# Stick-breaking weights as differences of suffix products, one weight tile per query tile in place, and transposed weights in ring slots

## The chip, the cores and the metric

One Trainium2 chip, of which this kernel uses one core. The metric is the time of one execution on the device in microseconds, as the median over runs. A core has five engines that run their own instruction streams in order: TensorE (PE, with its weight loads shown as PEld), VectorE (DVE), ScalarE (ACT), GpSimd (POOL) and SyncE (SP, which here issues all DMAs).

## The reference

One layer of a hybrid encoder. A prompt group of 1,024 tokens and a sample group of 32 tokens (with caches of 512 keys) go through the same weights. Each token is normed and projected to q, k, v and gate for two mixers of 8 heads x 64 each; mixer A is a softmax over a band, mixer B is stick-breaking attention. All is float32.

```python
def band_attention(q, k, v, q_pos, k_pos, bias_table):          # mixer A
    s = jnp.einsum('bqhd,bkhd->bhqk', q, k).astype(jnp.float32) * ATTN_SCALE
    rel = jnp.clip(k_pos[None, :] - q_pos[:, None], -REL_CLIP, REL_CLIP) + REL_CLIP
    s = s + bias_table[:, rel].astype(jnp.float32)[None]
    ok = ...                                # own 64-token chunk and the 8 before it
    w = jax.nn.softmax(jnp.where(ok[None, None], s, NEG_INF), axis=-1)
    return jnp.einsum('bhqk,bkhd->bqhd', w, v)

def stick_breaking(q, k, v, q_pos, k_pos):                      # mixer B
    z = jnp.einsum('bqhd,bkhd->bhqk', q, k).astype(jnp.float32) * ATTN_SCALE
    causal = (k_pos[None, :] < q_pos[:, None])[None, None]
    log_beta = jax.nn.log_sigmoid(z)
    log_1m = jnp.where(causal, jax.nn.log_sigmoid(-z), 0.0)
    after = lax.cumsum(log_1m, axis=3, reverse=True) - log_1m
    w = jnp.where(causal, jnp.exp(log_beta + after), 0.0)
    return jnp.einsum('bhqk,bkhd->bqhd', w, v)

def finish(h, oa, ga, ob, gb, w_out, g_post, p, w_ple, w_ple_gate):
    y = jnp.concatenate([oa * jax.nn.silu(ga), ob * jax.nn.silu(gb)], axis=-1) @ w_out
    h = h + rmsnorm(y, g_post)
    return h + jax.nn.sigmoid(h @ w_ple_gate) * (p @ w_ple)
```

In mixer B the weight of key k is sigmoid(z_k) times the product of sigmoid(-z_j) over all later keys j. With S_k the suffix product of sigmoid(-z_j) over j >= k, that weight is also S_(k+1) - S_k, because sigmoid(z) = 1 - sigmoid(-z).

## The kernel before

Every float32 operand of a matmul is split into a high part in fp32r and a low part (the rest), and each product is made of two or three fp32r matmuls. The work runs in these steps:

1. Up to about 66 us: the inputs are normed and turned, an early part of the per-layer embedding is made, and the first head pair's q, k and v columns are projected.
2. From there to about 600 us: 8 stages, one for each pair of heads, in the order A0 B0 A1 B1 A2 B2 A3 B3. A stage weaves two streams: the attention of its pair (two heads, named for instance A00 and A01) and "dense" work, which is the projection of the next stage's columns (`mm_kB1` are the k columns of pair B1) and, in the last stage, of all gates. The sample group's attention (`PVsA0`, `PVsB0`, ...) is put into the stages of odd pairs.
3. After that the output projection and the gate product, each by a Strassen-like scheme.

A head's attention works on 8 query tiles of 128. For tile i, `scores(i)` multiplies q with the keys into one or two PSUM banks of tag "S" (three banks) and makes the weights: for B, DVE adds the causal mask, ACT takes sigmoid(-z) into `w0` (ring `om`) and sigmoid(z) into `w1` (ring `be`), DVE scans `w0` from the right to suffix products, and POOL multiplies the two; for A, DVE adds the bias and takes the maximum into `w0`, ACT takes the exponential into `w1`, and POOL normalises it. `weights_t(i)` comes two tiles later: PE transposes the 128x128 blocks of `w1` into banks of tag "T" (two banks), ACT copies the high part to `wTh`, DVE the low part to `wTl`. Tiles 4 and 6 of each A head (`ROUND`) are turned by DVE and DMAs through a scratch in DRAM instead, and come back in four DMAs of 32 partitions each. `values(g)` then multiplies the values with the turned weights of four query tiles (g is 0 or 1; PV of tag "PV", one bank); its moving operand is a `Segments`, one run of 128 columns for each query tile. The sample's value product uses the same PV bank and keeps its operands in the four slots of tag "wr", into which the dense work's next weight columns are loaded as well.

`Arena` hands out columns of one big buffer in turn; a new tile waits for every user of the tiles that it overlaps. `wTh` and `wTl` are such rings of 33 x 128 columns, with one tile for each group of four query tiles.

None of this is the order on the chip. All operations go to a `Recorder` first, which notes for each what it must wait for: an operation on a view waits for earlier ones on an overlapping box of the same buffer. `Recorder.order` then lays out each engine's queue by simulating the kernel with estimated durations: whenever an engine is free it takes, of what is ready, the operation with the lowest key; attention's matmuls (class 0) go before dense ones (class 1). An operation on SP counts as landed some time after its issue. What a view knows of its box:

```python
    def rearrange(self, pattern, **sizes):
        ...
        return View(self.buf, self.steps + (("rearrange", pattern, sizes),), self.box, [None] * len(shape), shape)
```

A rearranged view keeps the box that it had, and an index into it afterwards doesn't make the box smaller, since its dimensions are None.

Almost every instruction is issued from one place of the recorder, so the profile gives them all line 450; they are told apart by the names of their tiles.

Of the kernel before, what the change touches and what calls it, by code (L numbers as in the profile page):

```python
# [8 lines left out]
F32 = mybir.dt.float32  # L9
# [21 lines left out]
ROUND = {"A": ((4,),(6,)), "B": ()}  # L31
# [127 lines left out]
class Segments:  # L159


    def __init__(self, buf, start, step, n):
        self.buf, self.start, self.step, self.n = buf, start, step, n
        self.shape = [buf.shape[0], n, P]
        self.box = (buf.box[0], (start, start + (n - 1) * step + P))

    def get(self):
        base = self.buf.get()[:, self.start:self.start + P]
        return bass.AP(tensor=base.tensor, offset=base.offset, ap=[base.ap[0], [self.step, self.n], [1, P]])
# [83 lines left out]

class Engine:
# [9 lines left out]
class Recorder:  # L264
# [43 lines left out]
    def add(self, eng, what, args, kw):  # L308
        writes, reads = [], []
        method = what[1] if isinstance(what, tuple) else ""  # L310
        for i, a in enumerate(args):
            if isinstance(a, (View, Raw, Segments)):
                (writes if i == 0 or (method == "tensor_tensor_reduce" and i == 7) else reads).append(a)
        for k, a in kw.items():
            if isinstance(a, (View, Raw, Segments)):
                (writes if k in ("out", "accum_out") else reads).append(a)
        o = self.node(eng, what, args, kw, set())
        for mine, write in ((reads, False), (writes, True)):
            for v in mine:
                b = v.buf  # L320
                hit = False
                for other, box, wrote in b.uses:
                    if other is not o and (write or wrote) and all(p < y and x < q for (p, q), (x, y) in zip(v.box, box)):
# [6 lines left out]
                b.uses.append((o, v.box, write))  # L330
        o.busy, o.late = self.cost(eng, method, args, kw, writes, reads)
        o.shared = eng == "POOL"
        if eng == "DVE":
            sbuf = [v for v in reads if isinstance(v, (View, Segments)) and not v.buf.psum and v.free() > 4]
            o.shared = len(sbuf) > 1 or (method == "tensor_copy" and len(sbuf) == 1 and not writes[0].buf.psum)

    @staticmethod
    def cost(eng, method, args, kw, writes, reads):
# [3 lines left out]
        psum = any(isinstance(v, (View, Segments)) and v.buf.psum for v in reads)  # L342
# [97 lines left out]
    def emit(self, tc):  # L440
        ops = self.order()
        with tc.manual_schedule():
            for o in ops:
# [3 lines left out]
                args = [a.get() if isinstance(a, (View, Raw, Segments)) else a for a in o.args]  # L447
                kw = {k: a.get() if isinstance(a, (View, Raw, Segments)) else a for k, a in o.kw.items()}
# [7 lines left out]
def stream_step(  # L456
# [58 lines left out]
    ringh, ringl = (Arena(rec, at, x, 33 * P, F32R) for x in ("wTh", "wTl"))  # L515
# [26 lines left out]
    def ensure(j):  # L542
# [6 lines left out]
        if j == 2:  # L549
            pair = [ringl.tile([P, 2, 4, P], f"w{x}_{kind}{p}") for x in "hl"]  # L550
# [14 lines left out]
    def load_x(t):  # L565
        n = min(P, T - t * P)
        if t == 3:
            x34.append(at.tile([P, ringh.cols], F32, tag="wTh", name="x34")[:, 0:2 * D].rearrange("p (a c) -> p a c", a=2))
# [209 lines left out]
    def attention(ab, p, h):  # L778
# [15 lines left out]

        together = {i: g for g in ROUND[ab] for i in g}
        whole, done_with = {}, []

# [3 lines left out]
        def rooms(i):  # L801

            more = ab == "B"
            g = together.get(i, (i,))
            if g not in whole:
                n = sum(cost(x) for x in g) * P
                whole[g] = ring0.tile([P, n + more * len(g)], f"om{nm}_{i}"), ring1.tile([P, n], f"be{nm}_{i}")
            k, n = g.index(i), cost(i) * P
            a = sum(cost(x) for x in g[:k]) * P
            w0, w1 = whole[g]  # L810
            return w0[:, a + more * k:a + more * k + n + more], w1[:, a:a + n]

        def scores(i):
# [5 lines left out]
            w0, w1 = rooms(i)  # L819
# [8 lines left out]
            if ab == "B":  # L828
# [3 lines left out]
                nc.gpsimd.memset(w0[:, n:n + 1], 1.0)  # L832
                for a, b, s in pieces:
                    nc.scalar.activation(w0[:, a:b], s, AF.Sigmoid, scale=-1.0)
                for a, b, s in pieces:
                    nc.scalar.activation(w1[:, a:b], s, AF.Sigmoid)
                for a, b, s in reversed(pieces):
                    rev = w0[:, a + 1:b + 1][:, ::-1]
                    nc.vector.tensor_tensor_scan(rev, rev, s, 1.0 if b == n else w0[:, b + 1:b + 2], ALU.mult, ALU.bypass)
                nc.gpsimd.tensor_tensor(w1[:, 0:n], w1[:, 0:n], w0[:, 1:n + 1], ALU.mult)  # L840
            else:
                m = small.tile([P, 4], F32, tag="stat", name=f"stat{nm}_{i}", bufs=6)
                for j, (a, b, s) in enumerate(pieces):
                    nc.vector.tensor_tensor_reduce(
                        w0[:, a:b], s, box["bias"][:, n - b:n - a][:, ::-1], 1.0,
# [6 lines left out]
            state[i] = w0, w1  # L852

        wT = {}
# [5 lines left out]
        def weights_t(i):  # L860
            g = i // 4
            step, size = LAID[ab, g]
            if g not in wT:
                wT[g] = [x.tile([P, size * P], f"{x.name}{nm}_{g}") for x in (ringh, ringl)]
            b0 = lo_block(i)
            w0, w1 = state.pop(i)
            n = i + 1 - b0
            at_ = ((i - 4 * g) * step + b0) * P
            hi, lo = (x[:, at_:at_ + n * P] for x in wT[g])
            if i in together:  # L870

                group = together[i]
                done_with.append((i, hi, lo))
                if i != group[-1]:
                    return
                w0, w1 = whole[group]
                m = sum(cost(x) for x in group)
                first = {x: sum(cost(y) for y in group[:k]) for k, x in enumerate(group)}
                squares = w0[:, 0:m * P].rearrange("p (c b q) -> p b c q", c=4, q=32)
                for x, _, _ in done_with:  # L880
                    y = slice(first[x], first[x] + cost(x))
# [6 lines left out]
                turned = w1.rearrange("p (g b q) -> p g b q", g=4, q=32)  # L888
                for x, hi, lo in done_with:
                    src = turned[:, :, first[x]:first[x] + cost(x), :]  # L890
                    hi, lo = (y.rearrange("p (b g q) -> p g b q", g=4, q=32) for y in (hi, lo))
                    nc.scalar.copy(hi, src)
                    nc.vector.tensor_tensor(lo, src, f(hi), ALU.subtract)
                done_with.clear()
                return
            for b in range(0, n, 4):
                m = min(4, n - b)
                pt = psum("T", f"ptw{nm}_{i}_{b}")
                for x in range(m):
                    nc.tensor.transpose(pt[:, x * P:(x + 1) * P], w1[:, (b + x) * P:(b + x + 1) * P], ident)  # L900
                c = slice(b * P, (b + m) * P)
                nc.scalar.copy(hi[:, c], pt[:, 0:m * P])
                nc.vector.tensor_tensor(lo[:, c], pt[:, 0:m * P], f(hi[:, c]), ALU.subtract)
# [6 lines left out]
        def values(g):  # L910
# [36 lines left out]
    def sample_attention(ab, gi):  # L947
# [44 lines left out]
        def scores():  # L992
# [6 lines left out]
            w0 = ring0.tile([P, NK + 1], "w0" + nm)  # L999
            w1 = ring1.tile([P, NK], "w1" + nm)  # L1000
            if ab == "B":
                new = pieces[1][2][:, NK // 2 - NS:NK // 2]
                nc.vector.tensor_tensor(new, new, masks, ALU.add)
                nc.gpsimd.memset(w0[:, NK:NK + 1], 1.0)
                for a0, b0, s in pieces:
                    nc.scalar.activation(w0[:, a0:b0], s, AF.Sigmoid, scale=-1.0)
                for a0, b0, s in pieces:
                    nc.scalar.activation(w1[:, a0:b0], s, AF.Sigmoid)
                for a0, b0, s in reversed(pieces):
                    rev = w0[:, a0 + 1:b0 + 1][:, ::-1]  # L1010
                    nc.vector.tensor_tensor_scan(rev, rev, s, 1.0 if b0 == NK else w0[:, b0 + 1:b0 + 2], ALU.mult, ALU.bypass)
                nc.gpsimd.tensor_tensor(w1[:, 0:NK], w1[:, 0:NK], w0[:, 1:NK + 1], ALU.mult)
            else:
                m = small.tile([P, 4], F32, tag="stat", name="stat" + nm, bufs=6)
                for j, (a0, b0, s) in enumerate(pieces):
                    nc.vector.tensor_tensor_reduce(
                        w0[:, a0:b0], s, bx["bias"][:, NK - b0:NK - a0][:, ::-1], 1.0,
                        -3e38 if j == 0 else m[:, 0:1], ALU.add, ALU.max, m[:, j:j + 1])
                nc.vector.tensor_scalar(m[:, 2:3], m[:, 1:2], -1.0, None, ALU.mult)
                nc.scalar.activation(w1[:, 0:NK], w0[:, 0:NK], AF.Exp, bias=m[:, 2:3], accum_out=m[:, 3:4])  # L1020
                nc.vector.reciprocal(m[:, 3:4], m[:, 3:4])
                nc.gpsimd.tensor_scalar(w1[:, 0:NK], w1[:, 0:NK], m[:, 3:4], 1.0, ALU.mult, ALU.mult)
            bx["w1"] = w1
# [6 lines left out]
        def weights():  # L1030
            w1 = bx["w1"]
# [12 lines left out]
            for b in range(4):  # L1044
                nc.tensor.transpose(pt[:, b * P:(b + 1) * P], w1[:, b * P:(b + 1) * P], ident)
# [4 lines left out]
            nc.tensor.transpose(pt[0:NS, 0:P], w1[:, PAST:NK], ident)  # L1050
# [280 lines left out]
    ghl = ringl.tile([P, 2, D], "ghl")  # L1331
# [519 lines left out]
```

## Time and profile before

| | |
|---|---|
| median of 3 runs | 806.26 us (805.87 to 806.33) |
| profiled execution, first to last instruction (its span) | 802.6 us |
| its own time beside the span | not given apart; the median lies 3.66 us above the span |
| PE busy | 792.0 us, 99% of the span, 4,734 matmuls |
| weight loads busy | 731.4 us |
| DVE, ACT, POOL busy | 565.7, 539.5, 469.5 us |
| DMA | 146.32 MB, 61.3% of the 16 engines' span |

Busy times of groups are sums over their instructions. Matmuls are pipelined, so the sum of their own durations is above the time that PE needed for them. "Idle before" is the time that the engine stood idle just before the instructions of a group, with what ended it; idle time of an engine that is not the bottleneck costs nothing. A stretch's row gives its start and end, its length, and for PE, weight loads, DVE, ACT and POOL the busy time and the number of instructions, then the granted clock of PE, the DMA share and GB/s.

### The profile page before, as it was taken

What the parts mean: (1) busy time and instruction counts of PE and PEld (TensorE: products, weight loads), DVE (VectorE), ACT (ScalarE), POOL (GpSimd) and SP (SyncE); (2) the same over time, 40 slices, a digit from 0 to 9 for tenths busy, and PEclk for the clock granted to TensorE, in tenths of its full rate; (3) what the DMA queues carried; (4) which work ended last, traced back from release to release, by engine and by line L of the source; (5) the groups of instructions that cost most, each with busy time, mean ns of one, the idle gap of its engine ahead of it and who ended that gap; (6) DMA issues with size and microseconds to landing.
All of it is one profiled execution on the core that took longest, in us unless ns stands there. A gap on an engine that the chain in (4) does not pass through costs nothing.

```text
span 802.6 us, 14554 instructions
## 1 busy us (share of the span) xinstructions
PE 792.0 (99%) x4734; PEld 731.4 (91%) x4734; DVE 565.7 (70%) x1129; ACT 539.5 (67%) x1163; POOL 469.5 (58%) x554
## 2 busy tenths in 40 slices
PE   9999999999999999999999999999999999999997
PEld 7899999999999999999999899999998877888786
DVE  7627878777787888776787586854554786587655
ACT  6636787786586777776787577644437868876741
POOL 6625867795686866635473265554553448599613
PEclk9999999999999999999999999999999999999999
DMA  9419986538876565833325656344389957769634
GB/s 293 135 46 285 236 230 186 153 112 254 220 229 198 145 184 158 208 103 102 92 60 141 146 158 205 99 149 138 105 277 300 288 174 242 236 197 345 215 117 131
DMA packets 147390, 146.32 MB, mean 182 GB/s; under 512 B 37409, under 2 KB 109257, under 8 KB 147314
## 3 DMA queue, kind: packets, MB, share of 16 engines
q1 hardware_dynamic: 147314, 145.39, 61.3%
q8 instruction: 38, 0.62, 0.3%
q14 instruction: 38, 0.31, 0.1%
HBM read 90.78 MB, written 46.16 MB: 171 GB/s over the span
## 4 chain that ended last, share of the span: by engine, by line
PE 89%; DVE 3%; DMA 2%; POOL 2%; ACT 1%; issue 1%; SPq 1%; POOLq 0%; DVEq 0%; ACTq 0%
PE mm_gB L450 6%; PE mm_gA L450 6%; PE mm_kB L450 6%; PE mm_qB L450 6%; PE mm_qA L450 5%; PE mm_kA L450 5%; PE mm_vB L450 4%; PE PVB L450 4%; PE mm_vA L450 4%; PE SB L450 4%; PE ptwB L450 4%; PE SA L450 3%; PE PVA L450 3%; PE g0P L450 2%; PE g1P L450 2%; PE o1P L450 2%
## 5 line engine op out<-in xcount | busy, mean ns | idle before, releaser
L450 POOL TENSOR_TENSOR be<-be,om 128x512 f32<-128x512 f32 (+8 forms) x66 | 82.9, 1260 | 77.8 <-DVE om L450 43.9
L450 DVE TENSOR_TENSOR_SCAN om<-om,SB 128x384 f32<-128x384 f32 (+5 forms) x96 | 92.6, 968 | 21.9 <-ACT be L450 11.7
L450 POOL TENSOR_SCALAR be<-be,statA 128x640 f32<-128x640 f32 (+3 forms) x64 | 44.4, 698 | 44.4 <-DVE statA L450 35.8
L450 DVE TENSOR_TENSOR wTl<-ptwB,wTh 128x512 fp32r<-128x512 f32 (+3 forms) x96 | 50.8, 546 | 13.8 <-ACT wTh L450 12.4
L450 ACT ACTIVATE om<-SB 128x384 f32<-128x384 f32 (+5 forms) x96 | 47.4, 499 | 19.0 <-DVE SB L450 14.2
L450 ACT CAST wTh<-ptwB 128x512 fp32r<-128x512 f32 (+3 forms) x96 | 44.6, 483 | 14.5 <-PE ptwB L450 10.5
L450 ACT ACTIVATE be<-om,statA 128x640 f32<-128x640 f32 (+3 forms) x64 | 44.6, 698 | 11.2 <-DVE statA L450 9.6
L450 ACT ACTIVATE be<-SB 128x384 f32<-128x384 f32 (+5 forms) x96 | 46.8, 498 | 6.8 <-DVE om L450 6.3
L450 PE MATMUL ptwB<-ident,be 128*128 128x128 f32 x288 | 44.0, 273 | 0.1
L450 PEld LDWEIGHTS ptwB<-ident,be 128*128 128x128 f32 x288 | 34.9, 140 | 2.2 <-PE mm_vA L450 0.4
L450 DVE CUSTOM_DVE_ANT_0 om<-SA,biasA 128x320 f32<-128x320 f32 (+2 forms) x64 | 30.7, 480 | 5.3 <-PE SA L450 4.9
L450 PE MATMUL SB<-kdB,LB 128*128 128x384 f32 (+5 forms) x96 | 34.0, 357 | 0.3 <-DVE om L450 0.3
L450 ACT CAST wTh<-ptwA 128x512 fp32r<-128x512 f32 (+2 forms) x64 | 26.0, 429 | 12.0 <-PE ptwA L450 11.4
L450 DVE TENSOR_TENSOR wTl<-ptwA,wTh 128x512 fp32r<-128x512 f32 (+2 forms) x64 | 29.7, 482 | 4.9 <-ACT wTh L450 4.0
L450 PE MATMUL SB<-klB,LB 128*128 128x384 f32 (+5 forms) x96 | 32.9, 347 | 0.0
L450 PE MATMUL SA<-kdA,LA 128*128 128x320 f32 (+2 forms) x96 | 30.0, 319 | 1.1 <-DVE LA L450 0.8
L450 PE MATMUL SA<-klA,LA 128*128 128x320 f32 (+2 forms) x96 | 29.8, 319 | 0.0
L450 POOL TENSOR_TENSOR gB<-gB,gB 128x256 f32<-128x256 f32 x32 | 26.6, 848 | 0.7 <-DMA gB<-in_w_ple_gate_dram 0.4
L450 PE MATMUL ptwA<-ident,be 128*128 128x128 f32 x160 | 26.5, 274 | 0.0
L450 DVE TENSOR_TENSOR SB<-SB,maskb 128x128 f32<-128x128 f32 x64 | 18.0, 292 | 9.9 <-PE SB L450 8.0
L450 POOL TENSOR_TENSOR oB<-oB,oB 128x256 f32<-128x256 f32 x32 | 23.6, 754 | 1.4 <-DMA oB<-in_w_out_dram 1.3
L450 POOL TENSOR_TENSOR h<-h,x 128x512 f32<-128x512 f32 (+1 forms) x18 | 23.0, 1295 | 0.8 <-DVE h L450 0.8
(706 smaller groups left out, 2668.3 us busy)
## 6 DMA issues: line engine op xcount, KB each, us to landing
swapA<-om SPq DMA_DIRECT2D x16, 320.0 KB, 3.5
be<-swapA SPq DMA_DIRECT2D x64, 80.0 KB, 2.9
oB<-in_w_out_dram SPq DMA_DIRECT2D x16, 256.0 KB, 3.9
sum_dro<-oB SPq DMA_DIRECT2D x16, 256.0 KB, 2.9
gB<-in_w_ple_gate_dram SPq DMA_DIRECT2D x16, 256.0 KB, 3.7
sum_drg<-gB SPq DMA_DIRECT2D x16, 256.0 KB, 3.2
x<-in_x_prompt_dram SPq DMA_DIRECT2D x16, 256.0 KB, 4.1
h_dr<-h SPq DMA_DIRECT2D x8, 512.0 KB, 3.6
```

The lines of the kernel that those rows point to most:

```text
L450: getattr(getattr(tc.nc, o.what[0]), o.what[1])(*args, **kw)
```

## The change

- Mixer B: one array `w` of n+1 columns in place of `w0` and `w1`. ACT takes sigmoid(-z) only; DVE scans it in place; POOL forms `w[1:n+1] - w[0:n]` in place. The second sigmoid (96 ACT instructions, and 4 in the sample group) is gone.
- Mixer A: bias, exponential and normalising in place in `w`.
- Transposed weights: a `Ring` of 33 slots, laid out as 4 x 33 x 32 columns, with one tile for each query tile and not for each group of four. The value product reads them through a `Span`: for each query tile four runs of 32 columns.
- The A tiles that are turned by DMA (4 and 6) use a buffer `x` of ring `be`; the four DMAs land straight in the slot of the low part; ACT copies the high part from there, and POOL (not DVE) subtracts it in place.
- The early users of the two rings (`ghl`, a weight pair) get a tile of their own in the same place.

```diff
-ROUND = {"A": ((4,),(6,)), "B": ()}
+ROUND = {"A": (4, 6), "B": ()}
+SLOTS = 33
+LOE = "P"
...
+class Span:
...
+    def get(self):
+        base = self.ring.whole.real[:, 0, self.slot, :]
+        return bass.AP(tensor=base.tensor, offset=base.offset,
+                       ap=[base.ap[0], [self.step * 32, self.n], [self.ring.slots * 32, 4], [1, 32]])
...
+class Ring:
...
+    def tile(self, lo, n, name):
+        if self.whole is None:
+            self.whole = self.pool.tile([P, 4, self.slots, 32], F32R, tag=self.name, name=self.name)
+        hi = lo + n
+        b = Buf([P, 4, n, 32], F32R, self.pool, name=name)
...
-    ringh, ringl = (Arena(rec, at, x, 33 * P, F32R) for x in ("wTh", "wTl"))
+    ringh, ringl = (Ring(rec, at, x, SLOTS) for x in ("wTh", "wTl"))
+    early = at.tile([P, SLOTS * P], F32R, tag="wTl", name="early")
...
                 for a, b, s in pieces:
-                    nc.scalar.activation(w0[:, a:b], s, AF.Sigmoid, scale=-1.0)
-                for a, b, s in pieces:
-                    nc.scalar.activation(w1[:, a:b], s, AF.Sigmoid)
+                    nc.scalar.activation(w[:, a:b], s, AF.Sigmoid, scale=-1.0)
                 for a, b, s in reversed(pieces):
-                    rev = w0[:, a + 1:b + 1][:, ::-1]
-                    nc.vector.tensor_tensor_scan(rev, rev, s, 1.0 if b == n else w0[:, b + 1:b + 2], ALU.mult, ALU.bypass)
-                nc.gpsimd.tensor_tensor(w1[:, 0:n], w1[:, 0:n], w0[:, 1:n + 1], ALU.mult)
+                    rev = w[:, a:b][:, ::-1]
+                    nc.vector.tensor_tensor_scan(rev, rev, s, 1.0 if b == n else w[:, b:b + 1], ALU.mult, ALU.bypass)
+                nc.gpsimd.tensor_tensor(w[:, 0:n], w[:, 1:n + 1], w[:, 0:n], ALU.subtract)
...
-                nc.scalar.activation(w1[:, 0:n], w0[:, 0:n], AF.Exp, bias=m[:, 2:3], accum_out=m[:, 3:4])
+                nc.scalar.activation(w[:, 0:n], w[:, 0:n], AF.Exp, bias=m[:, 2:3], accum_out=m[:, 3:4])
...
-                nc.gpsimd.tensor_scalar(w1[:, 0:n], w1[:, 0:n], m[:, 3:4], 1.0, ALU.mult, ALU.mult)
+                nc.gpsimd.tensor_scalar(w[:, 0:n], w[:, 0:n], m[:, 3:4], 1.0, ALU.mult, ALU.mult)
...
-                    nc.vector.transpose(squares[:, y], w1[:, y.start * P:y.stop * P])
-                dr = scratch([P, m * P], f"swap{nm}_{i}")
-                dma(dr, w0[:, 0:m * P])
+            if i in ROUND[ab]:
+                x = ring1.tile([P, n * P], f"x{nm}_{i}")
+                nc.vector.transpose(x.rearrange("p (c b q) -> p b c q", c=4, q=32), w[:, 0:n * P])
+                dr = scratch([P, n * P], f"swap{nm}_{i}")
+                dma(dr, x)
+                landed = f(lo).rearrange("p g s q -> p g (s q)")
                 for c in range(4):
-                    x = dr[:, c * m * 32:(c + 1) * m * 32].rearrange("(g k) x -> k g x", k=32)
-                    dma(w1[32 * c:32 * c + 32].rearrange("k (g x) -> k g x", g=4), x)
...
-                    nc.scalar.copy(hi, src)
-                    nc.vector.tensor_tensor(lo, src, f(hi), ALU.subtract)
+                    dma(landed[32 * c:32 * c + 32], dr[:, c * n * 32:(c + 1) * n * 32].rearrange("(g k) x -> k g x", k=32))
+                nc.scalar.copy(hi, f(lo))
+                (nc.gpsimd if LOE == "P" else nc.vector).tensor_tensor(lo, f(lo), f(hi), ALU.subtract)
                 return
...
-                w = Segments(wT[g][half], c.start * step + b * P, step * P, (c.stop - c.start) // P)
+                i0, i1 = c.start // P, c.stop // P
+                w = Span((ringh, ringl)[half], [laid[4 * g + i][half] for i in range(i0, i1)], wT[g][half] + i0 * step + b, step, i1 - i0)
                 nc.tensor.matmul(acc[:, c], v2[:, b, :], w, start=(n == 0), stop=(n == len(todo) - 1))
```

More of the change, by code (lines that the diff above doesn't have):

```diff
@@ L333, in add @@
         if eng == "DVE":
-            sbuf = [v for v in reads if isinstance(v, (View, Segments)) and not v.buf.psum and v.free() > 4]
+            sbuf = [v for v in reads if isinstance(v, (View, Span)) and not v.buf.psum and v.free() > 4]
             o.shared = len(sbuf) > 1 or (method == "tensor_copy" and len(sbuf) == 1 and not writes[0].buf.psum)
@@ L549, in ensure @@
         if j == 2:
-            pair = [ringl.tile([P, 2, 4, P], f"w{x}_{kind}{p}") for x in "hl"]
+            pair = [early[:, 2 * D + x * 1024:2 * D + (x + 1) * 1024].rearrange("p (h k c) -> p h k c", h=2, k=4) for x in range(2)]
         for kh in range(2):
@@ L801, in rooms @@
         def rooms(i):
[L803 to L811, printed above, removed]
+            n = cost(i) * P
+            return ring0.tile([P, n + (ab == "B")], f"w{nm}_{i}")
         def scores(i):
@@ L863, in weights_t @@
             if g not in wT:
-                wT[g] = [x.tile([P, size * P], f"{x.name}{nm}_{g}") for x in (ringh, ringl)]
+                wT[g] = ringh.base(size), ringl.base(size)
             b0 = lo_block(i)
-            w0, w1 = state.pop(i)
+            w = state.pop(i)
             n = i + 1 - b0
[L868 to L881, printed above, removed]
-                    nc.vector.transpose(squares[:, y], w1[:, y.start * P:y.stop * P])
-                dr = scratch([P, m * P], f"swap{nm}_{i}")
-                dma(dr, w0[:, 0:m * P])
-                for c in range(4):
-                    x = dr[:, c * m * 32:(c + 1) * m * 32].rearrange("(g k) x -> k g x", k=32)
-                    dma(w1[32 * c:32 * c + 32].rearrange("k (g x) -> k g x", g=4), x)
[L888 to L891, printed above, removed]
-                    nc.scalar.copy(hi, src)
-                    nc.vector.tensor_tensor(lo, src, f(hi), ALU.subtract)
-                done_with.clear()
```

109 lines of the change are left out of this document (64 added, 45 removed).

## The prediction

> **What bounds the kernel now.** I read the page's busy line and the chain of work that ended last first, then the busy time by stretch, then who TensorE waited for, and only then groups of instructions.
>
> ```profile
> span 802.6 us, 14554 instructions
> PE 792.0 (99%) x4734; PEld 731.4 (91%) x4734; DVE 565.7 (70%) x1129; ACT 539.5 (67%) x1163; POOL 469.5 (58%) x554
> PE 89%; DVE 3%; DMA 2%; POOL 2%; ACT 1%; issue 1%; SPq 1%; POOLq 0%; DVEq 0%; ACTq 0%
> ```
> ```profile
> 0.00:66.00 66.00, 62.18 (x367) 56.79 (x368) 37.00 (x55) 34.98 (x68) 32.87 (x57) 1.00 0.53 160
> 66.00:100.00 34.00, 34.00 (x223) 33.47 (x223) 26.95 (x96) 23.95 (x55) 23.10 (x28) 1.00 0.97 274
> 100.00:200.00 100.00, 99.71 (x649) 96.14 (x648) 77.40 (x149) 76.23 (x168) 71.33 (x89) 1.00 0.64 186
> 200.00:250.00 50.00, 49.80 (x328) 48.20 (x327) 40.00 (x97) 34.31 (x79) 36.26 (x50) 1.00 0.80 224
> 250.00:450.00 200.00, 199.76 (x1300) 193.17 (x1299) 155.97 (x331) 149.38 (x330) 112.66 (x136) 1.00 0.52 137
> 450.00:470.00 20.00, 19.10 (x124) 17.69 (x124) 13.57 (x45) 12.32 (x27) 8.07 (x9) 1.00 0.33 85
> 470.00:600.00 130.00, 130.00 (x839) 127.38 (x838) 81.96 (x147) 71.70 (x164) 72.88 (x82) 1.00 0.56 170
> ```
>
> The second view gives, for each stretch, its length and then the busy time of PE, weight loads, DVE, ACT and POOL; the granted clock is 1.00 throughout. Attention runs from 66 to about 600 us. There PE is idle for 0.29 + 0.20 + 0.24 + 0.90 = 1.63 us out of 534. No other engine is above 80%. So an engine that gets less work is worth at most those 1.63 us, and whatever makes PE wait costs its full length. The span is 802.6 us; the median of the runs, 806.26, is 3.66 us above it, and I add that 3.66 to every span below. A measurement of this kernel can tell about 0.2% from no change: 1.6 us.
>
> **The change part by part.** PE's own work does not change: in the built program there are as many matmuls and transposes of each shape as before. The rest first in engine time.
>
> ```profile
> L450 ACT ACTIVATE be<-SB 128x384 f32<-128x384 f32 (+5 forms) x96 | 46.8, 498 | 6.8 <-DVE om L450 6.3 <-DVE wTl L450 0.6
> L450 DVE TENSOR_TENSOR_SCAN om<-om,SB 128x384 f32<-128x384 f32 (+5 forms) x96 | 92.6, 968 | 21.9 <-ACT be L450 11.7 <-ACT om L450 6.6 <-issue 1.0
> L450 DVE TENSOR_TENSOR wTl<-be,wTh 128x640 fp32r<-128x640 f32 x16 | 18.1, 1131 | 4.6 <-ACT wTh L450 4.2
> L450 POOL TENSOR_TENSOR gT<-raw,gT 128x512 fp32r<-128x512 f32 x11 | 15.0, 1373 | 1.8 <-ACT gT L450 1.8
> L450 POOL TENSOR_TENSOR be<-be,om 128x1024 f32<-128x1024 f32 x8 | 19.1, 2387 | 12.8 <-DVE om L450 8.2 <-PE mm_kA L450 3.4 <-ACT om L450 1.0
> ```
>
> The second sigmoid goes: ACT loses 96 x 0.498 us, 47 us (plus four small ones in the sample group). It stands on the chain of a B tile: DVE's scans waited 11.7 us in all for it, since both read the same scores. So a B tile's chain shortens, by up to the 0.5 us of one such sigmoid for each piece of scores. What hides that chain is PE's dense work, in which the attention steps are set; where this cover is full, as the idle times above say, a shorter chain is worth 0, and in all no more than the 1.63 us. The POOL product becomes a subtraction of the same size: 0. A's exponential in place: 0. Tiles 4 and 6 of each A head are turned by DMA; their low half moves from DVE (16 x 1.131) to POOL. POOL does a subtraction into fp32r at 1.373 us for 512 columns, so I estimate 1.373 x 640/512 = 1.7 us each, 27 us in all: POOL goes from 470 to about 497 us, still off the path as a sum. Finer release of ring slots (by tile, not by group of four) removes waits for slots; PE shows none, so 0.
>
> The value products now read their weights in runs of 32 columns instead of 128.
>
> ```profile
> 167.69 3.55 PE mm_vA L450 x22
> 178.00 0.44 PE ptwB L450 x4
> 180.13 3.09 PE PVB L450 x16
> ```
>
> From the chain in order of time: 22 matmuls of 352 contiguous columns took 3.55 us, 0.458 ns a column; transposes take 0.11 us each. The 16 matmuls of a second B value product, 6,656 columns in runs of 128 with 36 breaks, should take 3.05 and took 3.09: at most 1 ns a break. After the change 1,056 runs of 128 become four each: 3,168 more breaks, 0 to 3 us. I take 0, because 36 breaks are within the reading error, and keep the 3 for the range. The Trainium skill ("SBUF — State Buffer", section "Door 1: The DMA port swizzle") says that SBUF reads go at full rate as long as consecutive accesses fall into the same 16-byte line, which runs of 128 bytes do; by it the 3 us would fall away. No run here shows runs of 32 yet.
>
> **What does reach PE is the order.** The planner (`Recorder.order`) lays out every queue anew, and PE's order differs from the 447th matmul on. The four landing DMAs of a turned tile now write through `landed = f(lo).rearrange(...)`. A rearranged view forgets which partitions a slice covers, so the planner takes the four for overlapping writes and places each after the landing of the one before. In the built order they stand apart on SP, with other transfers between, where before they mostly stood together. So A's second value product moves back. In PE work from the start (0.458 ns a column, 0.11 us a transpose) it begins at 110 us instead of 93 in head A00, at 220 instead of 207 in A10, at 449 instead of 431 in A30. The one PV bank then makes the sample's A product late (PVsA0 at 224 instead of 212, PVsA1 at 456 instead of 445), and behind that product wait the next dense weights, whose slots it reads last. Three places in the new order are then thin.
>
> ```profile
> 229.65 0.28 PE L450 MATMUL PVsA<-newh,newl 128*128 128x256 f32 x1
> 229.77 0.32 PE L450 MATMUL mm_vB<-hnh,wl_vB 128*128 128x352 f32 x1
> 229.93 1.46 PE L450 MATMUL mm_vB<-hnl,wh_vB 128*128 128x352 f32 x8
> 230.43 0.20 DVE L450 COPY be<-PVsA 32x64 f32<-32x64 f32 x1
> 230.67 0.42 ACT L450 COPY be<-PVsA 32x64 f32<-32x64 f32 x2 [0.51 <-DVE be L450]
> 231.12 0.22 DVE L450 COPY be<-PVsA 32x64 f32<-32x64 f32 x1 [0.41 <-ACT be L450]
> 231.46 0.71 PEld L450 LDWEIGHTS PVA<-wTh,v2A 128*128 128x128 f32 x4 [0.36 <-PE mm_vB L450]
> ```
>
> First, PVsA0 is followed at once by a transpose of its copied diagonal and by the next value product in the same bank. In the timeline of before the sample product ended at 229.93, its four copies at 231.34, and the next product in the bank loaded at 231.46: 1.53 us, with 9 dense matmuls (1.45 us by the spacing above) as cover. In the new order the cover is one transpose that itself waits for the copies. Price 1.4 us, at PVsA0 and again at PVsA1: 2.8.
>
> ```profile
> L450 ACT COPY otA<-PVA 64x512 f32<-64x512 f32 x16 | 9.3, 582 | 14.7 <-PE PVA L450 14.5
> L450 DVE TENSOR_TENSOR otA<-PVA,otA 64x512 f32<-64x512 f32 x16 | 11.0, 687 | 8.3 <-ACT otA L450 8.1
> L450 ACT CAST wTh<-ptwB 128x128 fp32r<-128x128 f32 x16 | 4.3, 266 | 0.2
> L450 DVE TENSOR_TENSOR wTl<-ptwB,wTh 128x128 fp32r<-128x128 f32 x16 | 4.5, 279 | 0.2
> wr_kA<-in_w_in_dram SPq DMA_DIRECT2D x8, 256.0 KB, 5.1
> wr_gA<-in_w_in_dram SPq DMA_DIRECT2D x8, 256.0 KB, 4.0
> ```
>
> Second, behind it come seven small transposes over two T banks with no dense work between. From the value product's end: ACT's copy 0.58, DVE's sum 0.69, DVE's low half 0.28 = 1.55 before the bank of `ptwA11_7` is free for `ptwB10_0`; PE has 3 transposes, 0.33, to do. Shortfall 1.2, and the next bank turns (0.27 + 0.28 each against 0.2 to 0.3 of work) add about 0.8: 2.0 at A1. At A3 four S matmuls (0.76) stand between as well: about 0.5. A second reckoning bounds both: the weights of the next dense columns are issued when the sample product has read their slot and land 5.1 us (kA) or 4.0 us (gA) later; from the end of the sample product to the first dense matmul the new order holds 2.7 us of PE work at both places (8.8 and 10.6 before). That gives 2.4 and 1.3 us at the least against 3.4 and 1.9 by the banks; they run side by side, so the larger counts.
>
> ```profile
> L450 DVE TENSOR_TENSOR SB<-SB,maskb 128x128 f32<-128x128 f32 x64 | 18.0, 292 | 9.9 <-PE SB L450 8.0
> L450 ACT ACTIVATE om<-SB 128x512 f32<-128x512 f32 x24 | 14.6, 607 | 5.4 <-DVE SB L450 4.7 <-POOL be L450 0.6
> L450 DVE TENSOR_TENSOR_SCAN om<-om,SB 128x512 f32<-128x512 f32 x24 | 29.7, 1237 | 7.3 <-ACT be L450 5.4 <-ACT om L450 1.5
> ```
>
> Third, tile 7 of head B01. Mask 0.29, sigmoid of the last piece 0.61, two scans 2 x 1.24, POOL's 2.39: 5.8 us from the last score matmul to the first transpose. The new order holds 16 dense matmuls, 9 transposes and 2,560 columns of scores: 4.7 us. Before, no tile 7 had under 7.6. Shortfall 1.1.
>
> Sum: 2.8 + 2.0 + 0.5 + 1.1 = 6.4, less the 1.6 of idle time that belonged to the old order: +4.8 us. Forecast 806.26 + 4.8 = **811.1 us** (span 807.4). With the first place alone: 2.8 - 1.6, 807.5. With all of it, the old idle kept and 3 us of slower reading: 806.3 + 6.4 + 3 = 815.7.
>
> **Rivals.** *Faster: the lighter ACT pays.* The shorter chain fills the idle time of before, and the thin places are covered because their chains run faster without 47 us of sigmoids in ACT's queue. For it: the 11.7 us for which the scans waited are gone; against it: the chains priced above hold none of the removed instructions. Price: 806.26 - 1.6 = 804.6, the most that PE's idle time allows. It decides if PE's idle time from 66 to 600 us stays near zero. Chance 0.10.
>
> *No change: the thin places bite half.* If the copies and the bank turns start earlier than planned, half of 6.4 less 1.6 remains: 806.3 + 1.6 = 807.9 at the top. Chance 0.13. What speaks against it is that the cover is counted in PE's own order. A rule of the Trainium skill ("TensorE: Matmul & The Clock Gate", Part 2, "What happens when you issue a matmul") says that only weight loads are pulled ahead and that matmuls stay in program order, so nothing passes a waiting one; the 0.36 us without a load before the last row of that timeline agrees.
>
> *Slower than forecast: POOL's low half is late.* The first low matmul of A's second product follows its first high one by 0.9 to 3.5 us of PE work in the new order, and needs 1.7 us of POOL after ACT's copy. With one 2.39 us product ahead in POOL's queue it needs 4.1, and most of the eight heads miss by 0.6 to 3.2; at half of them 7 us: 818. It decides if POOL's queue is full when the landing comes. Chance 0.12.
>
> *It doesn't do what it says*: slots are no wait of PE's now, so finer release was worth 0 already; this is inside the sum.
>
> **How the numbers follow.** Forecast's mechanism 0.65, faster 0.10, none 0.13, POOL 0.12. Range 805 to 817: it drops most of the faster rival and the end of POOL's, and holds the rest with the 3 us of the reads. Faster by over 0.2%: 0.10; within: 0.14; slower: 0.76 (a little of the forecast's low end lies within).
>
> **What would show it.** Right: PE's busy time unchanged within 3 us, idle time from 66 to 600 us at 6 to 8 us, most of it near 165 to 185, 225 to 245 and 460 to 485 us, with waits of PE for DVE's copies of PVsA, for T banks and for the dense weights; ACT 47 us less, POOL some 27 more. Wrong: idle time under 2 us there (the rivals above), or PE busy time up by more than 3 us at the same count (the reads), or waits of the value products for POOL's wTl (the POOL rival).

## The result, and the profile after

The changed kernel takes 826.05 us (median of 4 runs, 824.23 to 828.07), the kernel before 806.19 in the same comparison: ratio 1.0235, 95% interval 1.0201 to 1.0269, so 19.9 us slower. The forecast was 811.1 with a range of 805 to 817. The sign and the cause were right, and the forecast of 4.8 us was a quarter of what came. The profiled execution took 828.07 us, 1.77 above its span. In every run whose span is on record the time lies 1.7 to 2.0 us above it, so the 3.66 us that the prediction added to spans are too much: the profiled execution of the kernel before will have taken about 804.4 us (an estimate, 802.6 + 1.8), 1.9 us less than the median. The changed kernel's is 2.0 us above its median. So the two spans lie 23.7 us apart, where the medians lie 19.9 apart.

First the page of the changed kernel: span, busy times and the chain that ended last.

```profile
span 826.3 us, 14362 instructions
PE 801.3 (97%) x4734; PEld 736.0 (89%) x4734; DVE 552.7 (67%) x1113; ACT 502.7 (61%) x1063; POOL 491.1 (59%) x570
PE 85%; DMA 5%; DVE 3%; ACT 2%; POOL 2%; SPq 1%; issue 1%; ACTq 0%; DVEq 0%; POOLq 0%
```

ACT has 37 us less to do, DVE 13 less, POOL 22 more, and the number of matmuls is the same, yet the span is 23.7 us longer. In the chain, DMA went from 2% to 5%. Then the same stretches as in the prediction (length; busy time of PE, weight loads, DVE, ACT, POOL; granted clock, DMA share, GB/s):

```profile
0.00:66.00 66.00, 61.30 (x364) 55.30 (x364) 36.59 (x54) 34.97 (x68) 32.97 (x57) 1.00 0.51 158
66.00:100.00 34.00, 32.77 (x212) 32.02 (x213) 25.82 (x86) 21.50 (x51) 21.58 (x26) 1.00 0.96 265
100.00:200.00 100.00, 97.57 (x615) 93.56 (x614) 67.31 (x129) 61.17 (x125) 72.38 (x84) 0.98 0.59 171
200.00:250.00 50.00, 46.03 (x294) 42.52 (x292) 41.32 (x110) 33.37 (x76) 38.52 (x55) 1.00 0.70 199
250.00:450.00 200.00, 196.35 (x1254) 188.61 (x1255) 138.63 (x304) 125.91 (x272) 118.80 (x138) 0.99 0.53 140
450.00:470.00 20.00, 20.00 (x138) 19.65 (x137) 14.93 (x47) 13.84 (x33) 7.12 (x12) 1.00 0.59 140
470.00:600.00 130.00, 126.15 (x804) 121.77 (x804) 82.39 (x162) 67.34 (x148) 71.76 (x81) 0.99 0.49 138
```

PE's idle time from 66 to 600 us is 1.23 + 2.43 + 3.97 + 3.65 + 0.00 + 3.85 = 15.1 us, where it was 1.6. And the granted clock, 1.00 everywhere before, is below it in three stretches. Windows of 3.41 us show why (length, PE busy, clock, DMA share, GB/s):

```profile
185.14:188.55 3.41, 1.37 (x9) 1.00 0.83 219
188.55:191.96 3.41, 3.02 (x10) 0.50 0.54 150
191.96:195.38 3.42, 3.42 (x26) 1.00 0.42 142
249.99:253.41 3.42, 2.16 (x13) 1.00 0.87 235
256.82:260.23 3.41, 1.99 (x12) 1.00 0.88 193
260.23:263.64 3.41, 3.41 (x13) 0.50 0.70 219
516.23:519.64 3.41, 1.03 (x6) 1.00 0.80 248
519.64:523.06 3.42, 3.42 (x14) 0.50 0.03 10
```

Three times PE stood idle for a good part of such a window (busy 40%, 58% and 30% of it), and each time the next window ran at half clock. The window at 249.99, busy for 63%, had no such effect. What a half-clock window costs is seen in the timeline:

```profile
261.48 1.38 PE L491 MATMUL mm_kA<-hnh,wl_kA 128*128 128x352 f32 x4
262.65 1.26 PE L491 MATMUL mm_kA<-hnh,wh_kA 128*128 128x352 f32 x4
```

Four matmuls of 352 columns from 261.48 to 262.65, 0.293 us each where 22 of them took 0.161 each before. A window of 3.41 us then does 3.41 x 0.161 / 0.293 = 1.87 us of work, so three of them lose some 4.6 us (an estimate from these two spacings).

That accounts for the longer span: 13.5 us more idle time in attention, 9.3 more of PE busy time (4.6 for the three half-clock windows; most of the other 4.7 are probably the longer records of matmuls that start after a break, as the third place below shows them; no run separates them), and 0.9 us more idle time before 66 us.

### The profile page after: what moved, and what is told of

The parts are those of the page before. It is cut to its first block, busy times and chain, and to the rows that moved or that the text cites. A ratio compares the mean times of both kernels' runs of the same rounds, so it can differ in the third digit from the quotient of the medians.

```text
span 826.3 us, 14362 instructions
## 1 busy us (share of the span) xinstructions
PE 801.3 (97%) x4734; PEld 736.0 (89%) x4734; DVE 552.7 (67%) x1113; ACT 502.7 (61%) x1063; POOL 491.1 (59%) x570
## 4 chain that ended last, share of the span: by engine, by line
PE 85%; DMA 5%; DVE 3%; ACT 2%; POOL 2%; SPq 1%; issue 1%; ACTq 0%; DVEq 0%; POOLq 0%
PE mm_gB L491 6%; PE mm_kA L491 5%; PE mm_qA L491 5%; PE mm_vB L491 5%; PE mm_vA L491 5%; PE mm_qB L491 5%; PE mm_kB L491 5%; PE mm_gA L491 4%; PE PVB L491 4%; PE SB L491 4%; PE ptwB L491 3%; PE PVA L491 3%; PE SA L491 3%; PE g1P L491 2%; PE o1P L491 2%; PE o3P L491 2%
## 5 line engine op out<-in xcount | busy, mean ns | idle before, releaser
L491 POOL TENSOR_TENSOR om<-om 128x1024 f32<-128x1024 f32 (+8 forms) x66 | 80.0, 1214 | 56.5 <-DVE om L491 40.2
L491 DVE TENSOR_TENSOR_SCAN om<-om,SB 128x384 f32<-128x384 f32 (+5 forms) x96 | 91.8, 967 | 15.1 <-ACT om L491 13.9
L491 POOL TENSOR_SCALAR om<-om,statA 128x640 f32<-128x640 f32 (+2 forms) x64 | 47.3, 742 | 37.7 <-DVE statA L491 30.2
L491 ACT ACTIVATE om<-SB 128x384 f32<-128x384 f32 (+5 forms) x96 | 44.1, 495 | 18.7 <-DVE SB L491 11.0
L491 ACT ACTIVATE om<-om,statA 128x640 f32<-128x640 f32 (+2 forms) x64 | 44.5, 696 | 15.7 <-DVE statA L491 15.3
L491 PE MATMUL ptwB<-ident,om 128*128 128x128 f32 x288 | 45.7, 275 | 1.8 <-ACT vtB L491 0.9
L491 PEld LDWEIGHTS ptwB<-ident,om 128*128 128x128 f32 x288 | 35.6, 141 | 4.8 <-issue 1.7
L491 DVE TENSOR_TENSOR SB<-SB,maskb 128x128 f32<-128x128 f32 x64 | 18.1, 292 | 18.4 <-PE SB L491 17.8
L491 POOL TENSOR_TENSOR gB<-gB,gB 128x256 f32<-128x256 f32 x32 | 23.7, 758 | 10.4 <-issue 7.3
L491 POOL TENSOR_TENSOR wTl<-wTl,wTh 128x640 fp32r<-128x640 f32 x16 | 26.2, 1644 | 5.6 <-ACT wTh L491 5.4
L491 PE MATMUL ptwA<-ident,om 128*128 128x128 f32 x160 | 25.5, 273 | 0.0
L491 PEld LDWEIGHTS SA<-kdA,LA 128*128 128x128 f32 x96 | 17.9, 189 | 7.4 <-DVE statA L491 3.5
```

The lines of the kernel that those rows point to most:

```text
L491: getattr(getattr(tc.nc, o.what[0]), o.what[1])(*args, **kw)
```

## Where the idle time is

Who PE waited for, in the changed kernel (us in total, times, longest):

```profile
PE PVA L491 <- ACT wTh L491: 2.6, 2, 2.4
PE SA L491 <- DVE statA L491: 2.5, 4, 1.1
PE SA L491 <- DVE om L491: 2.0, 2, 1.3
PE PVA L491 <- POOL wTl L491: 1.2, 1, 1.2
PE mm_kA L491 <- ACT wh_kA L491: 0.9, 2, 0.7
```

These waits are spread over many places. Three places of its timeline carry the reading (start, duration, and in brackets the idle time before, with what ended it). The first is the landing of a turned tile late in the last A head:

```profile
504.24 0.32 SPq L491 DMA_DIRECT2D wTl<-swapA  x1
507.57 0.43 SPq L491 DMA_DIRECT2D wTl<-swapA  x1
510.60 0.50 SPq L491 DMA_DIRECT2D wTl<-swapA  x1
518.45 0.72 ACT L491 CAST wTh<-wTl 128x640 fp32r<-128x640 f32 x1 [4.01 <-DMA wTl<-swapA]
519.23 1.11 PE L491 MATMUL PVA<-wTh,v2A 128*128 128x512 f32 x4 [2.38 <-ACT wTh L491]
```

The last three landings of the tile are issued some 3 us apart, the last one landed 7.8 us after its issue, ACT waited 4.0 us for it, and PE waited for ACT. This wait set off the third half-clock window. Over all 16 turned tiles, the time from a tile's first landing issue to its fourth is 8.57 us in the median; before, it was 1.74. The same tile in the kernel before, all four landings in one row:

```profile
480.62 1.85 SPq L450 DMA_DIRECT2D be<-swapA  x4
```

The second place is the start of head A10's scores, where a B tile's scans stand ahead on DVE:

```profile
185.84 2.54 DVE L491 TENSOR_TENSOR_SCAN om<-om,SB 128x512 f32<-128x512 f32 x2 [0.97 <-ACT om L491]
187.11 0.44 PE L491 MATMUL SA<-kdA,LA 128*128 128x384 f32 x1 [1.35 <-DVE om L491]
188.43 0.71 PE L491 MATMUL SA<-kdA,LA 128*128 128x512 f32 x1 [0.70 <-DVE om L491]
```

PE's next score matmuls need S banks that these two scans free one after the other. The scans are those of tile 7 of head B01. The third is the stretch from 240 to 259 us, which has no dense matmul at all:

```profile
250.46 0.39 PE L491 MATMUL PVsA<-Vl2sA,whsA 128*128 128x256 f32 x1 [0.75 <-DVE Vl2sA L491]
252.21 0.33 PE L491 MATMUL ptosA<-ident,be 128*128 128x128 f32 x1 [0.54 <-DVE be L491]
255.43 0.33 PE L491 MATMUL ptwB<-ident,om 128*128 128x128 f32 x1 [0.44 <-ACT vtB L491]
257.55 0.63 PE L491 MATMUL ptwB<-ident,om 128*128 128x128 f32 x4 [0.50 <-DVE wTl L491]
258.91 0.92 PE L491 MATMUL mm_kA<-hnh,wh_kA 128*128 128x352 f32 x4 [0.73 <-ACT wh_kA L491]
```

Here the sample's product (PVsA) waits for its own operands, then come the PV bank, the T banks one by one, and at last the dense weights, whose slots that product had held: each chain in the open, one after the other. From 239.94 to 258.91 us, 18.97 us, PE has 9.4 us of work, at the prediction's 0.458 ns a column and 0.11 us a transpose. It stands idle for 6.0 us. The other 3.5 us are in the records: a transpose that starts after a break has a record of 0.33 us, and PE is busy for all of it.

## The experiments

Each edit is against the kernel named. "Theory" and "Rival" in the expectations are named in brackets there; in the first three the theory is that PE's order, spoilt by landings which the planner takes for overlapping writes, makes the loss. Medians are of the runs of each kernel, ratios against the kernel before on the same chip, with 95% intervals.

**1. The landings sliced before they are rearranged** (changed kernel):

```diff
-                landed = f(lo).rearrange("p g s q -> p g (s q)")
                 for c in range(4):
-                    dma(landed[32 * c:32 * c + 32], dr[...])
+                    landed = f(lo)[32 * c:32 * c + 32].rearrange("p g s q -> p g (s q)")
+                    dma(landed, dr[...])
```

> The changed kernel, with one edit: each landing DMA slices its 32 partitions before it rearranges, so the planner sees four writes that do not overlap. Theory (serial landings): A's second value products move back to where before had them, the longest stretch of PE's order in attention without dense matmuls shrinks from 9.4 to 4.3 us, so 806 to 810 us, PE idle from 66 to 600 us under 4 us and no stretch at half clock. Rival (the weights now live in one arena, om, from score to turning, and that arena of 3,076 columns is what holds scores back; or POOL's low half): the landings are a side show, 818 to 826 us.

Measured: 807.92 us, ratio 1.0019 (1.0009 to 1.0029). The bytes, engines and instructions are those of the change; only the order differs. 18.1 of the 19.9 us are gone. The stretch of attention in it, and then a row of its timeline for SP:

```profile
66.00:600.00 534.00, 528.92 (x3431) 513.40 (x3432) 392.93 (x847) 333.31 (x721) 343.13 (x406) 1.00 0.61 168
```
```profile
470.96 1.75 SPq L491 DMA_DIRECT2D wTl<-swapA  x3
```

PE's idle time in attention is 5.1 us (the expectation said under 4), the clock stays at 1.00, and the landings stand together again (1.8 us from first to fourth issue in the median). The longest stretch of PE's order without dense matmuls holds 4.4 us of work, close to the expected 4.3.

**2. The opposite edit in the kernel before**: rearrange first, slice afterwards.

```diff
+                landed = w1.rearrange("k (g x) -> k g x", g=4)
                 for c in range(4):
                     ...
-                    dma(w1[32 * c:32 * c + 32].rearrange("k (g x) -> k g x", g=4), x)
+                    dma(landed[32 * c:32 * c + 32], x)
```

> The kernel before, with one edit: its landing DMAs rearrange first and slice afterwards, as in the change. The transfers are the same. Theory (serial landings): PVA10_1 moves from 207 to 217 us and PVA30_1 from 431 to 452 us of PE work, stretches without dense matmuls of 8 to 10 us appear at 217, 257 and 452, so 815 to 830 us, with PE idle there of 8 us or more. Rival (one arena, POOL): 806 us within 1.6, as nothing else is changed.

Measured: 869.87 us, ratio 1.0775 (1.0744 to 1.0806). The direction is as expected and the size is more than twice the expected. None of the other parts of the change is in this kernel, so the landings alone can do it. Its stretch of attention, which now reaches to 666 us, and the longest wait in its timeline:

```profile
66.00:666.00 600.00, 563.31 (x3471) 538.03 (x3472) 400.31 (x865) 382.16 (x832) 327.44 (x391) 0.95 0.54 152
```
```profile
538.46 1.35 PE L450 MATMUL PVA<-wTh,v2A 128*128 128x512 f32 x4 [4.88 <-DVE be L450]
```

PE is idle for 36.7 us there, and the mean clock is 0.95. The landings spread over 10.9 us in the median. Why this kernel loses three times what the change does is seen only in part. Its clock record has 16 windows at half clock, which at the 1.5 us of the estimate above cost up to 25 us, and it has 35 us more idle time than the kernel before. Why so much more was not separated; its turned tiles land in the arena `be`, which holds all the weights of that kernel, and not in a slot of their own.

**3. The low half of turned tiles back on DVE** (changed kernel, `LOE = "D"`):

> The changed kernel with the low half of turned tiles subtracted on DVE again, as before. Theory (serial landings): PE's order stays as in the change (PVA10_1 at 219, PVsA0 at 223 us, the same 9.4 us without dense matmuls), so 821 to 829 us. Rival (POOL's low half is late): PE's wait for POOL's wTl goes and with it the loss, 808 to 812 us.

Measured: 818.42 us, ratio 1.0152 (1.0131 to 1.0172). Neither expectation holds: 7.6 us come back, though PE's order has the same 9.4 us without dense matmuls. That POOL's subtraction costs this much is not shown: the planner laid out a new order here too (PE's differs from that of the change from about its 685th matmul on), and gone are not only PE's one wait for POOL (1.2 us) but also most of the waits at 187 to 190 us and the one at 519 us. PE's idle time in attention is still 2.11 + 4.24 + 1.53 + 2.75 = 10.6 us (66 to 200, 200 to 250, 250 to 450 and 450 to 600 us), and two windows ran at half clock.

**4. The second sigmoid taken out alone** (kernel before; scans in place of the shifted ones, POOL subtracts into `w1`):

```diff
-                for a, b, s in pieces:
-                    nc.scalar.activation(w1[:, a:b], s, AF.Sigmoid)
...
-                nc.gpsimd.tensor_tensor(w1[:, 0:n], w1[:, 0:n], w0[:, 1:n + 1], ALU.mult)
+                nc.gpsimd.tensor_tensor(w1[:, 0:n], w0[:, 1:n + 1], w0[:, 0:n], ALU.subtract)
```

> The kernel before with the second sigmoid taken out alone: B's weights are differences of neighbouring suffix products, still written to the be arena; A, slots and reads as before. ACT loses 47 us. Theory (PE's order decides): the order changes from the 731st matmul, with one stretch of 6.6 us without dense matmuls at 200 us: 806 to 810 us. Rival (a lighter ACT pays): 804.6 us or less.

Measured: 810.15 us, ratio 1.0048 (1.0031 to 1.0064). Taking 34 us of ACT's busy time away (539.5 to 505.1 on its page) made the kernel 3.9 us slower, 0.15 us above what the theory allowed. The planner laid everything out anew; as ACT has less to do and the work of PE is the same, the new order must be the worse one.

**5. Landings sliced first, and the low half on DVE**:

> The changed kernel with the landings sliced first (807.92 us alone) and the low half of turned tiles on DVE. Theory (POOL's low half costs only where the late landings leave it no time): within 2 us of 807.9, so 806 to 810 us. Rival (POOL's low half costs some 7 us by itself, as 826.05 to 818.42 would say): 800 to 803 us.

Measured: 805.72 us, ratio 0.9985 (0.9970 to 1.0001). Against experiment 1 the same edit is worth 2.2 us, where it was 7.6 with the late landings. A little beyond what was expected at its low end; the rival's 800 to 803 is out.

**6. No tile turned by DMA** (landings sliced first, `ROUND` empty for A: 80 more transposes):

> The changed kernel with no tile turned by DMA: no landings at all, and 80 transposes more on PE, 80 x 0.109 = 8.7 us. Theory (late landings make the loss): no landing, no loss, 806 + 8.7, so 812 to 817 us, faster than the 826 of the change though PE has more to do, and no stretch at half clock. Rival (the loss comes from elsewhere in the change and the order of e1 was luck): over 826 us.

Measured: 811.72 us, ratio 1.0052 (1.0029 to 1.0076), just under the expected 812. PE has more to do and the kernel is 14 us faster than the change.

```profile
66.00:600.00 534.00, 532.42 (x3490) 518.21 (x3491) 390.69 (x859) 329.52 (x732) 315.13 (x388) 1.00 0.52 145
```

With no landings PE is idle for 1.58 us in attention, as before the change.

**7. Landings sliced first, and the arenas cut 4,100 to 2,360 columns**:

> The changed kernel with the landings sliced first and the two arenas cut differently, om 4,100 columns (3,076) and be 2,360 (3,384). Theory (om is no bound once the landings are together): 806 to 810 us, as 807.9. Rival (weights that stay in om until they are turned hold the next scores back): 803 to 806 us. The planner's order changes from the 131st matmul, so a miss of a few us either way is the order's.

Measured: 812.01 us, ratio 1.0057 (1.0037 to 1.0078): both missed. PE's idle time in attention is as in experiment 1 (534 - 528.78 = 5.2 us), and 1.4 us more of it falls before 66 us (60.80 busy there against 62.22). A larger `om` brings nothing; whether the smaller `be` or chance in the order costs the rest stays open.

**8. Landings sliced first, and the second sigmoid back**:

> The changed kernel with the landings sliced first and the second sigmoid of B's 64 prompt tiles back (into the be arena, multiplied on POOL). ACT gets back about 45 us. Theory (ACT's time is off the path): within 2 us of 807.9, 806 to 810 us. Rival (the removed sigmoid pays a few us that the landings had hidden): 810 us or more.

Measured: 808.79 us, ratio 1.0018 (1.0002 to 1.0035). With 34 us more on ACT than experiment 1 (538.8 against 505.1 busy) the time is 0.9 us higher. Each was compared with the kernel before on a chip of its own, and by these ratios (1.0018 and 1.0019) there is no difference.

**9 to 11. A wider margin in the planner**: `MARGIN`, by which the planner delays a PE instruction behind its operands, at 600 ns and not 400; in the kernel of experiment 5, in the kernel before, and in that of experiment 5 with the second sigmoid back.

> The changed kernel with the landings sliced first, the low half on DVE and the planner's margin before a PE instruction at 600 ns (400). The least cover in PE's order goes up: from the last score matmul of a bank to the first of its next use 1.46 us at the least (0.58 in the change, 1.38 without the margin). Theory (short covers in PE's order make the idle time, engine work does not): 802 to 805 us. Rival (the cover does nothing, PE's idle time is where an operand is late): 805.7 us or more.

> The kernel before with the margin at 600 ns alone. If the margin helps by itself, 803 to 805.5 us; then what e9 gains over 806.2 is not the change's. If it doesn't, 806 to 808 us.

> As e9, with the second sigmoid of B's prompt tiles back. Theory (ACT is off the path): within 2 us of e9, and the difference is the order's. Rival (with the order mended, a shorter B chain pays): slower than e9 by more than 2 us.

Measured: 805.16 us (ratio 0.9984, 0.9971 to 0.9997), 808.41 (1.0034, 1.0017 to 1.0052) and 806.61 (0.9997, 0.9985 to 1.0009). Experiment 9 is the fastest kernel here, 1.2 us below the one before, which is less than the 0.2% that the prediction called measurable; it missed its expected 802 to 805 by a little. In the changed kernel the margin gives 0.6 us by the medians and nothing by the ratios (0.9984 against 0.9985 in experiment 5); in the kernel before it costs 2.1 us, so it is no gain by itself. The second sigmoid costs 1.45 us in this order.

## Why the prediction was right in its direction and a quarter of the size

**The bound: right.** PE is the bound, and less work elsewhere pays almost nothing: the second sigmoid is worth at most 0.9 and 1.45 us (experiments 8 and 11), within the 1.63 us that the prediction allowed. Its 47 us in the sum of records were some 34 us of ACT's busy time.

**The reads in runs of 32: right.** B's value products with the most columns, in the groups of the kernel before and then of the changed one:

```profile
L450 PE MATMUL PVB<-wTl,v2B 128*128 128x512 f32 x48 | 16.1, 412 | 0.0
L491 PE MATMUL PVB<-wTl,v2B 128*128 128x512 f32 x48 | 15.9, 412 | 0.0
```

The mean is 412 ns in both. The cost taken, 0 of a bound of 3 us, holds.

**POOL's low half: the duration right, its price open.**

```profile
L491 POOL TENSOR_TENSOR wTl<-wTl,wTh 128x640 fp32r<-128x640 f32 x16 | 26.2, 1644 | 5.6 <-ACT wTh L491 5.4
```

1.64 us each, 26 us in all, against an estimate of 1.7 and 27. The profile shows one wait of PE for it (1.2 us), but with the subtraction on DVE 7.6 us come back (experiment 3), and 2.2 with the landings in time (experiment 5). The rival said 7 us over the forecast and had a chance of 0.12, as an alternative to the order. In fact the two come together. How much of the 7.6 and the 2.2 is POOL's time, and how much the new order that the planner lays out for the edit, was not separated.

**The false overlap of the landings: right.** It is the cause: 18.1 of 19.9 us go when they are sliced first (experiment 1), and the same edit in reverse slows the kernel before by 63.6 us (experiment 2). A new order alone moves the time too, by 2 to 4 us in experiments 4, 7 and 10, but every kernel without the false overlap lies between 805.2 and 812.0 us, and the three that have it lie at 818.4 or more. Whether PE then loses more by its own order or by operands that land late was not separated.

**The sum over thin places: wrong, and this is the step that failed.** What it priced came nearly as priced; it left out most of the places. In its own terms a place loses the time that passes there less PE's work (0.458 ns a column, 0.11 us a transpose). Worked out so from the starts of PE's instructions in the trace, the priced places lost 7.3 us where the sum had 6.4. Places for which it had no term lost some 15 us, and the half-clock windows 4.5. Less some 3 us of losses that belonged to the old order, this makes the 23.7 us between the two spans.
- The first place (PV bank after the sample product, 1.4 us each) lost 1.3 us at 252 us and 1.3 at 497.5.
- The second (T banks, 2.0 at A1 and 0.5 at A3) lost 2.5 us from 254.1 to 257.9 and 0.9 at 501.6. But the prediction let the late dense weights run beside it and counted the larger. In the timeline they follow each other: after the last T bank the wait for `wh_kA` lost another 1.35 us.
- The third (tile 7 of head B01, 1.1 us) lost nothing at its transposes. Its two scans instead held up A10's scores, by the S banks, at 187 us.
- Not in the sum at all: those scores behind B's scans (3.5 us up to 190), scores of head A11 at 219.5 to 224 (2.3), the value products behind a late landing and POOL at 240 to 244 (2.2), the sample product behind its own operands at 247 to 251 (2.5), the landing of 7.8 us (2.5 at 519), 0.6 us at 500, and 1.4 us at 92, a wait that experiments 1, 3 and 5 have as well.

The sum looked for covers shorter than a chain measured when no queue was in the way. In an order without dense matmuls, every chain is open, and the queues of DVE and SP add to each.

**The clock: no term.** The prediction saw 1.00 throughout and priced idle time at its own length. Three half-clock windows added some 4.6 us by the spacing above. The Trainium skill ("TensorE: Matmul & The Clock Gate", Part 1, "What's actually happening") says that the clock is either full or half and is set by a free-running window of 3,413 ns, with half clock after an idle window. The trace agrees on the half and on the 3.41 us. It differs on the condition: by an idle window there would have been no such loss here, but windows in which PE was busy for 58% already led to half clock, while one with 2.16 of 3.42 us (63%) didn't. Nor is the limit a busy share between these two, as a window of experiment 5 and the one behind it show:

```profile
478.47:481.88 3.41, 1.84 (x13) 1.00 0.96 275
481.88:485.29 3.41, 3.41 (x23) 1.00 0.69 186
```

There PE was busy for 54%, and the clock stayed.

**What would show it** was named with one flaw: PE's busy time up by more than 3 us was to mean slower reads. It rose by 9.3 us for other reasons: a matmul at half clock counts as busy for longer, and so does one that starts after a break. The idle time was to be 6 to 8 us and came to 15.1. PE's waits for the copies of PVsA, the T banks and the dense weights came as named, and so did one for POOL's `wTl`, which was to be a sign of the rival.

Of the whole, then: the false overlap 18.1 us, the low half on POOL another 2.2 (taken away in the other order 7.6 for the low half, then 12.7 for the overlap), and the three parts that the change is named for, without these two, leave 805.72 against 806.2: no difference that this measurement can tell (experiment 5).

## What to carry to other kernels

When a planner sets the order, an edit that only touches how a view is written can cost more than all the arithmetic it saves: look first at which operations it newly believes to depend on each other, and at the spread of their issue times on the queue. A kernel that keeps its matmul engine at 99% lives on cover; when a stretch of the new order has none (here 9.4 us of PE's work without a dense matmul), price the chains in it one after another, with the queues that they stand in, and not only the thinnest places. And idle time there can cost more than its length: three windows in which PE was partly idle were each followed by one at half clock here.

## What was not expected of the hardware

Partial idleness halves the clock: windows of 3.41 us with PE busy for 30%, 40% and 58% were each followed by one at 0.50, and the clock was back at 1.00 one window later. In experiment 3 the windows that led to half clock were busy for 36% and 52% (worked out from the matmuls of its trace). As the window of 54% in experiment 5 kept the full clock, PE's busy share alone does not say when the clock falls; what does is not settled here.

A landing of 80 KB that takes 3.2 us in the median of the 64 in the changed kernel took 7.8 us once, at the end of a stretch of the queue in which 8 other transfers were issued between the tile's second landing and its last. That one landing cost 2.4 us of waiting and a window at half clock. What made it slow was not tested. The trace is of one execution, the longest of the four (824.23, 824.33, 827.76 and 828.07 us); whether the shorter ones have this landing is not on record.
